# Seven-product FFN: gate sums, a weight sum and a cast listed sooner, other PSUM banks for group 0's down product, last rows of h split by token halves

## Chip, cores and metric

The kernel runs on one core of a Trainium2 chip. Its time is the device time of one execution in microseconds (us); three timed runs of the kernel before are at hand, and one execution under the profiler.

## The reference

One decoder layer on 512 tokens of width 1024, in float32: an FFN, a token-mixing part, a second FFN, a gated embedding (PLE) and a norm.

```python
def rmsnorm(x, g):
    xf = x.astype(jnp.float32)
    y = xf * lax.rsqrt(jnp.mean(xf * xf, axis=-1, keepdims=True) + EPS)
    return (y * g.astype(jnp.float32)).astype(x.dtype)

def swiglu(x, w_gate, w_up, w_down):
    return (jax.nn.silu(x @ w_gate) * (x @ w_up)) @ w_down
...
        h = h + 0.5 * swiglu(rmsnorm(h, ffn1_norm[i]), ffn1_w_gate[i], ffn1_w_up[i], ffn1_w_down[i])
        n = rmsnorm(h, mix_norm[i])
        proj = n @ w_in[i]
...
        h = h + jnp.concatenate([ya, yb], axis=-1) @ w_out[i]
        h = h + 0.5 * swiglu(rmsnorm(h, ffn2_norm[i]), ffn2_w_gate[i], ffn2_w_up[i], ffn2_w_down[i])
        gate = jax.nn.sigmoid(rmsnorm(h, ple_norm[i]) @ ple_w_gate[i] + ple_b_gate[i])
        h = h + gate * (p[i] @ ple_w_proj[i])
    return rmsnorm(h, final_norm)
```

The hidden width of each FFN, D_FF, is 2816, or 11 groups of 256.

## The kernel before

**Float32 by parts.** Each operand of a product is split into a rounded part (hi) and a remainder (lo). A weight tile that a DMA has brought in (raw, rawb or s) is cast to `whi` on ScalarE (ACT, line 515) and `wlo = raw - whi` is made on VectorE (DVE, line 519); TensorE (PE) then adds three products, whi with x's hi, whi with x's lo, wlo with x's hi.

**The FFN's groups.** Group 0 is computed plainly (`plain_steps`). Groups 1 to 10 compute gate and up halves of two token halves with seven block products instead of eight (`Group.steps`), one step each, 24 matmuls of 128x256 (line 731), in the order 1, 7, 6, 4, 5, 2, 3 (group 1 of the first FFN is "turned": 1, 7, 2, 6, 4, 5, 3). Three PSUM accumulators belong to a group: x (steps 1, 2), q (steps 7, 4), both from the three "mm" banks, and a (steps 6, 5, 3), of which there are two, used by alternate groups. Step 1 ends with a copy of x into a, the seed (line 853); p7 and u2 are kept copies (lines 857, 861). The weights of step 6 are w11 plus a sum s1, those of step 3 that plus w12. These sums are made in place on DVE (line 741: `add(w11.raw, self.s1)`, `add(w11.raw, w12.raw)`); s1 itself and step 7's weights are made by accumulating DMAs on GpSimd's (POOL's) queue (lines 749 and 746).

**The gate.** `gate_sum(0)` (line 874, G<-mm,u) needs q after step 4 and u2; `gate_sum(1)` (line 874, G<-a,p) needs a after step 5 and p7. Step 3 adds into the same a bank, so PE's step 3 waits for `gate_sum(1)`. `gate(half)` scales (line 879, DVE) and applies Silu (line 881, ACT); `times_r` (line 885), and `finish` (line 890, at even groups of the second half also line 894) follow.

**Order.** PE, ACT, DVE and SyncE execute what the program lists, in that order. `run` walks through the steps and lists, around a step's product, the cast of the step two ahead, what follows the products before it (`after`), the wlo of later steps (`split`), weight sums (`sums`) and the tasks attached by `also` (`post`). The first FFN's first steps are listed by hand, in the string `ENTRY` (product11 is step 3 of the turned group; after9 belongs to its step 4, and so on).

**Down products.** Group 0's part of the down product takes four steps of two products each (`down`, matmuls at line 231, sums into h at line 930): steps 0 and 2 write two small-pool banks "sm", steps 1 and 3 two "mm" banks. The first block of the rest of the down product (`blocks_down`, 35 steps, line 1096), also on seven products, writes sm. It forms its own operands from G on ACT and DVE (line 1023).

**The rows of h.** At the end of each FFN, h is finished row block by row block. Each of the eight is scaled by the next norm and split (`scaled_split`: ACT line 199, DVE line 200), squared (line 273, ACT) and summed (line 274, GpSimd or DVE) for the norm. Blocks 4 to 7 are done one by one while step 3 of `blocks_down` runs; blocks 0 to 3 follow after its last product (`upper_done`), all 512 tokens at a time. Only the second token half of blocks 0 to 3 is changed by that last product (`add_to(0, k, 1, "a", ...)`); the first half is final at the first step of it (`add_to(0, 1, 0, "x", ...)`).

```python
        def upper_done():
            for k in range(2):
                add_to(0, k, 1, "a", ALU.add)
                yield
            yield from parts_of_h(range(NP))
```

What follows the second FFN is the PLE gate: products with x (line 231), a sum over the squares (line 284), the norm's scale (lines 240 to 308), and its spread over partitions (line 321).

## Time and profile before

| | |
|---|---|
| timed runs | 1071.28, 1065.8, 1065.92 us; median 1065.92 |
| profiled execution | 1069.35 us; span of its profile 1067.6 us |
| granted TensorE clock, mean | 0.991 |
| DVE idle for ACT's whi, line 519 of raw tiles | 64.9 us |
| ACT idle ahead of the Silu, line 881 | 134.9 us |

A row of a timeline has the start from the span's begin, the length in us, the engine, line and operation, what it writes and reads, and in brackets the engine's idle time ahead of it with what ended that. A row of the waits has who waited for whom, us in total, how often, and the longest. A row of windows has the stretch, its length, the busy time of PE, PE's weight loads, DVE, ACT and POOL with the counts of instructions, then the granted clock, the DMA engines' busy share and GB/s. A row of DMA issues ends with the KB of each and the median us from issue to landing.

### The profile page before, as it was taken

The page shows a single profiled execution, that of the slowest core. Times are in us where ns is not written, and L with a number is a line of the kernel's source. Part 1 is how long each engine was busy: PE and PEld are TensorE (multiplying, and loading weights), DVE is VectorE, ACT ScalarE, POOL GpSimd, SP SyncE. Part 2 cuts the span into 40 slices and gives each one's busy share as a digit, 9 for nine tenths or more (in the row PEclk, how much of TensorE's full clock was granted, in tenths as well). Part 3 has the DMA queues.
Part 4 walks back from the last instruction along what each step waited for, and adds up shares of the span by engine and source line. Part 5 has one row for each costly group of instructions (what it writes and reads, how often), then busy time and mean ns, then how long its engine had stood idle before and what let it go on. Part 6 is the DMA issues. An engine that isn't in the chain of part 4 may idle for free. (4 is left out here: it accounts for less than half of the span.)

```text
span 1067.6 us, 18352 instructions
## 1 busy us (share of the span) xinstructions
PE 1027.9 (96%) x7472; PEld 958.0 (90%) x7472; DVE 848.2 (79%) x1104; ACT 574.2 (54%) x764; POOL 151.9 (14%) x145
## 2 busy tenths in 40 slices
PE   9989999999999999999999999999999999999996
PEld 7889999998999899888888888889999998999886
DVE  7968778778898787776998757677778778998866
ACT  7644544545666465575754434454444446576654
POOL 0101001000320300134333000000010000330311
PEclk9989999999999999999999999999999999999988
DMA  9957667626992143444532325755676543995312
GB/s 339 314 138 212 183 159 204 177 64 240 226 233 63 58 126 90 155 144 133 148 110 72 107 86 185 173 144 163 185 192 178 167 130 144 263 211 152 131 47 80
DMA packets 51765, 168.90 MB, mean 158 GB/s; under 512 B 5856, under 2 KB 6368, under 8 KB 51680
## 3 DMA queue, kind: packets, MB, share of 16 engines
q1 hardware_dynamic: 38864, 123.61, 34.2%
q0 software_dynamic: 11520, 41.95, 20.6%
q10 hardware_dynamic: 1296, 2.16, 0.6%
q8 instruction: 58, 0.95, 0.4%
q14 instruction: 27, 0.22, 0.1%
HBM read 163.44 MB, written 4.26 MB: 157 GB/s over the span
## 5 line engine op out<-in xcount | busy, mean ns | idle before, releaser
L519 DVE TENSOR_TENSOR wlo<-raw,whi 128x1024 fp32r<-128x1024 f32 (+3 forms) x166 | 201.1, 1212 | 65.1 <-ACT whi L515 64.9
L515 ACT CAST whi<-raw 128x1024 fp32r<-128x1024 f32 (+3 forms) x166 | 166.8, 1011 | 127.1 <-PE a L217 24.0
L731 PE MATMUL mm<-xfb,whi 128*128 128x256 f32 x960 | 163.9, 275 | 0.0
L731 PEld LDWEIGHTS mm<-xfb,whi 128*128 128x128 f32 x960 | 145.8, 192 | 0.0
L731 PE MATMUL mm<-xfb,wlo 128*128 128x256 f32 x480 | 132.1, 275 | 0.0
L519 DVE TENSOR_TENSOR wlo<-rawb,whi 128x1024 fp32r<-128x1024 f32 x76 | 92.9, 1222 | 49.2 <-ACT whi L515 49.1
L731 PE MATMUL a<-xfb,whi 128*128 128x256 f32 x640 | 115.7, 284 | 14.5 <-ACT G L881 10.7
L731 PEld LDWEIGHTS a<-xfb,whi 128*128 128x128 f32 x640 | 98.8, 195 | 21.0 <-ACT G L881 13.7
L515 ACT CAST whi<-rawb 128x1024 fp32r<-128x1024 f32 x76 | 79.4, 1047 | 55.4 <-DVE rawb L741 31.7
L881 ACT ACTIVATE G<-G 128x512 f32<-128x512 f32 x40 | 25.2, 630 | 134.9 <-DVE G L879 134.9
L731 PE MATMUL a<-xfb,wlo 128*128 128x256 f32 x320 | 90.9, 284 | 5.4 <-DVE wlo L519 5.4
L731 PEld LDWEIGHTS mm<-xfb,wlo 128*128 128x128 f32 x480 | 92.2, 192 | 0.1
L1096 PE MATMUL a<-xfb,whi 128*128 128x256 f32 x480 | 80.7, 275 | 0.0
L746 POOL DMA_DIRECT2D raw<-in_ffn_gu x20 | 17.2, 861 | 430.0 <-DMA raw<-in_ffn_gu 254.4
L1096 PEld LDWEIGHTS a<-xfb,whi 128*128 128x128 f32 x480 | 72.8, 192 | 0.0
L731 PEld LDWEIGHTS a<-xfb,wlo 128*128 128x128 f32 x320 | 62.3, 195 | 8.9 <-DVE wlo L519 8.9
L217 PE MATMUL sm<-x,whi 128*128 128x512 f32 x224 | 68.4, 387 | 0.0
L1096 PE MATMUL a<-xfb,wlo 128*128 128x256 f32 x240 | 66.0, 275 | 0.0
L1096 PE MATMUL sm<-xfb,whi 128*128 128x256 f32 x320 | 54.3, 276 | 2.4 <-DVE h L930 2.4
L274 POOL TENSOR_TENSOR ssum<-ssum,tmp 128x512 f32<-128x512 f32 x26 | 38.6, 1484 | 117.6 <-ACT tmp L273 116.9
L731 PE MATMUL a<-xfa,whi 128*128 128x256 f32 x320 | 54.7, 275 | 0.1
L731 PE MATMUL mm<-xfa,whi 128*128 128x256 f32 x320 | 54.7, 275 | 0.0
(411 smaller groups left out, 2642.8 us busy)
## 6 DMA issues: line engine op xcount, KB each, us to landing
raw<-in_ffn_gu SPq DMA_DIRECT2D x56, 512.0 KB, 4.7
rawb<-in_ffn_gu SPq DMA_DIRECT2D x32, 512.0 KB, 7.6
raw<-in_w_in SPq DMA_DIRECT2D x28, 512.0 KB, 3.6
s<-in_ffn_gu SPq DMA_DIRECT2D x20, 512.0 KB, 5.9
raw<-in_ffn_gu POOLq DMA_DIRECT2D x20, 512.0 KB, 7.8
s<-in_ffn_gu POOLq DMA_DIRECT2D x20, 512.0 KB, 9.6
rawb<-in_ffn_dw POOLq DMA_DIRECT2D x18, 512.0 KB, 9.5
raw<-in_w_out SPq DMA_DIRECT2D x16, 512.0 KB, 3.3
```

Source lines behind the costliest of these rows:

```text
L217: nc.tensor.matmul(ps, w, turned(x), start=first and n == 0, stop=last and n == 2, skip_group_check=True)
L274: self.engines[i].tensor_tensor(self.totals[i], self.totals[i], sq, ALU.add)
L515: nc.scalar.copy(self.hi[:, c], self.raw[:, c])
L519: nc.vector.tensor_tensor(self.lo[:, c], self.raw[:, c], self.hi[:, c].bitcast(F32), ALU.subtract)
L731: nc.tensor.matmul(o, wt[:, c], turned(xt), start=fresh and p == m == n == 0, stop=last and n == 2, skip_group_check=True,)
L746: nc.gpsimd.dma_start(w21.raw, self.src[0], accum_op=ALU.add)
L881: nc.scalar.activation(t, t, AF.Silu)
L1096: nc.tensor.matmul(o, wt[:, c], xt, start=i in (1, 7) and t == jj == n == d % 2 == 0, stop=t == nt - 1 and jj == 1 and d % 2 == 1 and n == ...
```

## The change

The change edits the listing at six places. No product is added or taken away, and PE's order stays the same but for the names of banks.

1. The two gate sums of a group stand together, and the scaling and Silu of half 0 behind them.
2. The weight sum for step 3 is listed after step 6's product (ahead of step 2's wlo) instead of among the `sums` two steps later.
3. Step 6's cast becomes a task of its own (`cast`), which `run` lists ahead of what follows step 3 of the group before (its Silu of half 1).
4. Group 0's down product uses mm and a for step 0, sm for step 1, mm for steps 2 and 3.
5. Blocks 0 to 3 of h are split, squared and summed by token halves: half 0 in `post` tasks of the last steps of `blocks_down`, half 1 where all was before. ACT has 16 rows more in the program, DVE 8, GpSimd 8.
6. In `ENTRY`, the weight sum of step 3 of the turned group comes right behind after9, and its cast and wlo (split12) ahead of product11.

The core of the diff:

```diff
-split10 split10.1 load13 product9 split11 load14 product10 after9 after10
-after10.1:1 product11 after11
+split10 split10.1 load13 product9 split11 load14 product10 after9 after9.1 after10
+after10.1:1 split12 product11 after11
...
-    def scaled_split(h, name, k):
-
-        hi = sb("x", dt=F32R)
-        lo = sb("x", dt=F32R)
-        nc.scalar.activation(hi, h[k], AF.Copy, scale=col(name, k))
+    def scaled_split(h, name, k, tok=slice(0, T), to=None):
+
+        hi, lo = to or (sb("x", dt=F32R), sb("x", dt=F32R))
+        nc.scalar.activation(hi[:, tok], h[k][:, tok], AF.Copy, scale=col(name, k))
         nc.vector.scalar_tensor_tensor(
-            lo, h[k], col(name, k), hi.bitcast(F32), ALU.mult, ALU.subtract
+            lo[:, tok], h[k][:, tok], col(name, k), hi[:, tok].bitcast(F32), ALU.mult, ALU.subtract
         )
...
-                gates[0] = gates[0][0],
-                gates[1] = gates[1][0][:1],
+                gates[0] = [lambda: self.gate_sum(0)],
+                gates[1] = [lambda: self.gate_sum(1), lambda: self.gate(0)],
...
-                    (6, w11, None, "a", False, (), lambda: add(w11.raw, self.s1), (self.keep_u2,)),
+                    (6, w11, None, "a", False, (), lambda: add(w11.raw, self.s1), ([self.keep_u2, lambda: add(w11.raw, w12.raw)],)),
...
-                    (3, w11, None, "a", False, (), lambda: add(w11.raw, w12.raw), (lambda: self.finish(1),) if self.turned else ([up, lambda: self.gate(1)],)),
+                    (3, w11, None, "a", False, (), None, (lambda: self.finish(1),) if self.turned else ([up, lambda: self.gate(1)],)),
...
+            alone = i == 6 and not self.turned
+
             def split():
-                yield from w.split_by_engine(self.s1 if raw else None, kept=parts)
+                if alone:
+                    w.low()
+                    parts[0] = w.hi, w.lo
+                else:
+                    yield from w.split_by_engine(self.s1 if raw else None, kept=parts)
...
+            if alone:
+                s.cast = w.cast
...
-                    ps[d] = bank("mm", 3) if i % 2 else sm_ps()
+                    ps[d] = sm_ps() if i == 1 else acc_ps() if d == D_ORDER[1] else bank("mm", 3)
...
-            yield from parts_of_h(range(NP))
+            yield from parts_of_h(range(NP), halves[1])
...
+        for t, ds in ((1, (0,)), (2, (1,)), (3, (2, 3))):
+            also(made[3][t], "post", lambda ds=ds: parts_of_h(ds, halves[0]))
```

How this moves instructions is shown at three places. Rows give the line (in the changed kernel a line in this part of the code is up to 10 lower down or one higher up), the operation, what it writes and reads, and the tile's size.

DVE in group 8 of the first FFN, from step 2's wlo and the weight sum for step 3 to the scaling of half 1. mm_2104 is q, a_269 the group's a bank, rawb_2038 is w12, raw_249 is w11. Before:

```order
L519 TENSOR_TENSOR wlo_2201<-rawb_2038,whi_2200 128x1024
L741 TENSOR_TENSOR raw_249_1873<-raw_249_1873,rawb_2038 128x1024
L519 TENSOR_TENSOR wlo_2230<-raw_249_1873,whi_2229 128x1024
L874 TENSOR_TENSOR G_628<-mm_2104,u_283_2198 128x2x256
L879 SCALAR_TENSOR_TENSOR G_628<-G_628,rall_488 128x2x256
L874 TENSOR_TENSOR G_628<-a_269_2069,p_280_2167 128x2x256
L519 TENSOR_TENSOR wlo_2262<-rawb_2102,whi_2261 128x1024
L885 SCALAR_TENSOR_TENSOR G_628<-G_628,rall_488 128x2x256
L519 TENSOR_TENSOR wlo_2293<-raw_2135,whi_2292 128x1024
L741 TENSOR_TENSOR rawb_2102<-rawb_2102,s_278_2138 128x1024
L890 TENSOR_TENSOR G_628<-G_628,mm_2070 128x2x256
L879 SCALAR_TENSOR_TENSOR G_628<-G_628,rall_488 128x2x256
```

and in the changed kernel:

```order
L740 TENSOR_TENSOR raw_249_1873<-raw_249_1873,rawb_2038 128x1024
L518 TENSOR_TENSOR wlo_2202<-rawb_2038,whi_2201 128x1024
L518 TENSOR_TENSOR wlo_2230<-raw_249_1873,whi_2229 128x1024
L881 TENSOR_TENSOR G_629<-mm_2104,u_283_2198 128x2x256
L881 TENSOR_TENSOR G_629<-a_269_2069,p_280_2167 128x2x256
L886 SCALAR_TENSOR_TENSOR G_629<-G_629,rall_488 128x2x256
L518 TENSOR_TENSOR wlo_2262<-rawb_2102,whi_2261 128x1024
L892 SCALAR_TENSOR_TENSOR G_629<-G_629,rall_488 128x2x256
L518 TENSOR_TENSOR wlo_2293<-raw_2135,whi_2292 128x1024
L740 TENSOR_TENSOR rawb_2102<-rawb_2102,s_278_2138 128x1024
L897 TENSOR_TENSOR G_629<-G_629,mm_2070 128x2x256
L886 SCALAR_TENSOR_TENSOR G_629<-G_629,rall_488 128x2x256
```

The weight sum (raw_249 with rawb_2038) went ahead of step 2's wlo, and the sum that reads a_269 ahead of the scaling of half 0. ACT, in the same group and the next step 6 (raw_249 here is w11 with s1 added, its cast whi_2098 or whi_2095; the Silus are G). Before:

```order
L881 ACTIVATE G_628<-G_628 128x2x256
L515 CAST whi_2033<-raw_249_1873 128x1024
L515 CAST whi_2064<-raw_1906 128x1024
L881 ACTIVATE G_628<-G_628 128x2x256
L515 CAST whi_2098<-raw_249_1873 128x1024
L853 COPY a_269_2069<-mm_2070 128x512
```

and in the changed kernel:

```order
L888 ACTIVATE G_629<-G_629 128x2x256
L514 CAST whi_2033<-raw_249_1873 128x1024
L514 CAST whi_2064<-raw_1906 128x1024
L514 CAST whi_2095<-raw_249_1873 128x1024
L888 ACTIVATE G_629<-G_629 128x2x256
L860 COPY a_269_2069<-mm_2070 128x512
```

The cast of step 6's weights changed places with the Silu of half 1, and both stand ahead of the seed copy a_269. DVE at the entry, in group 1 of the first FFN, where rawb_171 is w11, mm_502 is q and a_98 the a bank. Before:

```order
L519 TENSOR_TENSOR wlo_587<-s_57_216,whi_586 128x1024
L874 TENSOR_TENSOR G_628<-mm_502,u_116_622 128x2x256
L879 SCALAR_TENSOR_TENSOR G_628<-G_628,rall_488 128x2x256
L874 TENSOR_TENSOR G_628<-a_98_458,p_107_553 128x2x256
L741 TENSOR_TENSOR rawb_171<-rawb_171,rawb_282 128x1024
L519 TENSOR_TENSOR wlo_658<-rawb_171,whi_657 128x1024
L519 TENSOR_TENSOR wlo_662<-raw_110_560,whi_661 128x1024
```

and in the changed kernel:

```order
L518 TENSOR_TENSOR wlo_587<-s_57_216,whi_586 128x1024
L740 TENSOR_TENSOR rawb_171<-rawb_171,rawb_282 128x1024
L881 TENSOR_TENSOR G_629<-mm_502,u_116_622 128x2x256
L886 SCALAR_TENSOR_TENSOR G_629<-G_629,rall_488 128x2x256
L518 TENSOR_TENSOR wlo_633<-rawb_171,whi_632 128x1024
L881 TENSOR_TENSOR G_629<-a_98_458,p_107_553 128x2x256
L518 TENSOR_TENSOR wlo_662<-raw_110_560,whi_661 128x1024
```

The weight sum moved from behind the second gate sum to ahead of the first, and its wlo to ahead of the second. Last, DVE in group 0's down product of the first FFN; h_94 to h_97 are parts of h, to which each of the four steps adds its two products, and sm, mm and a are the banks that are read. Before:

```order
L519 TENSOR_TENSOR wlo_2780<-raw_2625,whi_2779 128x512
L930 TENSOR_TENSOR h_94<-sm_2762,h_94 128x512
L930 TENSOR_TENSOR h_96<-sm_2769,h_96 128x512
L519 TENSOR_TENSOR wlo_2800<-raw_2658,whi_2799 128x512
L885 SCALAR_TENSOR_TENSOR G_628<-G_628,rall_488 128x2x256
L1023 TENSOR_TENSOR xfb_2804<-G_628,xfb_2804 128x1024
L930 TENSOR_TENSOR h_94<-mm_2783,h_94 128x512
L930 TENSOR_TENSOR h_96<-mm_2790,h_96 128x512
L519 TENSOR_TENSOR wlo_2822<-rawb_2660,whi_2821 128x1024
L890 TENSOR_TENSOR G_628<-G_628,a_317_2526 128x2x256
L894 TENSOR_TENSOR G_628<-G_628 128x512
L930 TENSOR_TENSOR h_95<-sm_2807,h_95 128x512
```

and in the changed kernel:

```order
L518 TENSOR_TENSOR wlo_2780<-raw_2625,whi_2779 128x512
L937 TENSOR_TENSOR h_94<-mm_2762,h_94 128x512
L937 TENSOR_TENSOR h_96<-a_347_2769,h_96 128x512
L518 TENSOR_TENSOR wlo_2800<-raw_2658,whi_2799 128x512
L892 SCALAR_TENSOR_TENSOR G_629<-G_629,rall_488 128x2x256
L1030 TENSOR_TENSOR xfb_2804<-G_629,xfb_2804 128x1024
L937 TENSOR_TENSOR h_94<-sm_2783,h_94 128x512
L937 TENSOR_TENSOR h_96<-sm_2790,h_96 128x512
L518 TENSOR_TENSOR wlo_2822<-rawb_2660,whi_2821 128x1024
L897 TENSOR_TENSOR G_629<-G_629,a_317_2526 128x2x256
L901 TENSOR_TENSOR G_629<-G_629 128x512
L937 TENSOR_TENSOR h_95<-mm_2807,h_95 128x512
```

No row moved here; only the banks changed. The fourth step's second product is mm_2838, and it lies in the bank of mm_2807 (three mm banks in turn: 2807, 2814, 2831), so its first matmul waits for the row h_95<-mm_2807.

More of the change, by code (lines that the diff above doesn't have):

```diff
@@ L263, in __init__, with add @@
             self.n = 0
-        def add(self, src):
+        def add(self, src, tok=slice(0, T)):
             i = self.n % len(self.engines)
@@ L271, in add @@
             else:
-                sq = tmp()
-                nc.scalar.activation(sq, src, AF.Square)
-                self.engines[i].tensor_tensor(self.totals[i], self.totals[i], sq, ALU.add)
+                sq, t = tmp()[:, tok], self.totals[i][:, tok]
+                nc.scalar.activation(sq, src[:, tok], AF.Square)
+                self.engines[i].tensor_tensor(t, t, sq, ALU.add)
         def sums(self, more=None):
@@ L696, in splitter, with done @@
         x += [None] * ND
-        def done(d):
-            x[d] = scaled_split(h, name, d)
+        def done(d, tok=slice(0, T)):
+            x[d] = scaled_split(h, name, d, tok, x[d])
         return done
@@ L1057, in seeds, with parts_of_h @@
                 yield
-        def parts_of_h(ds, then=None):
+        def parts_of_h(ds, tok=slice(0, T)):
             for d in ds:
-                after(d)
+                after(d, tok)
                 yield
-                out_norm.add(h[d])
+                out_norm.add(h[d], tok)
                 yield
```

## The prediction

> **What bounds the kernel now.** I read the page's busy shares first, then PE's waits, then two windows that hold the product groups (groups 2 to 10 of the first FFN, 1 to 10 of the second), and at last one group on the timeline.
>
> ```profile
> PE 1027.9 (96%) x7472; PEld 958.0 (90%) x7472; DVE 848.2 (79%) x1104; ACT 574.2 (54%) x764; POOL 151.9 (14%) x145
> PE a L731 <- ACT G L881: 10.7, 19, 2.2
> PE a L731 <- DVE wlo L519: 5.4, 18, 0.5
> ...
> 64.56:246.69 182.13, 175.21 (x1514) 170.70 (x1513) 139.46 (x154) 86.50 (x109) 12.65 (x15) 1.00 0.58 157
> 691.50:895.97 204.47, 195.00 (x1681) 189.75 (x1680) 159.98 (x182) 97.33 (x124) 13.77 (x16) 1.00 0.56 154
> ```
>
> TensorE (PE) is busy 96% of the span, so only its waiting can be won. The two wait rows have the count of the groups: 19 times "ACT G L881", 18 times wlo. Their idle (10.7 + 5.4) understates the loss, since ends of pipelined matmuls are modelled; starts are not. So I measure by starts. On PE, the first matmuls of steps 6 (191.26), 5, 2 and 3 of one group of the first FFN and of step 6 of the next (211.59):
>
> ```profile
> 191.26 0.38 PE L731 MATMUL a<-xfb,whi 128*128 128x256 f32 x1
> 197.28 0.39 PE L731 MATMUL a<-xfa,whi 128*128 128x256 f32 x2
> 199.96 0.39 PE L731 MATMUL mm<-xfb,whi 128*128 128x256 f32 x2
> 203.27 0.46 PE L731 MATMUL a<-xfb,whi 128*128 128x256 f32 x2 [0.47 <-ACT G L881]
> 211.59 0.49 PE L731 MATMUL a<-xfb,whi 128*128 128x256 f32 x2
> 212.37 0.38 PE L731 MATMUL a<-xfb,wlo 128*128 128x256 f32 x1 [0.29 <-DVE wlo L519]
> ```
>
> A step that waits for nothing takes 199.96 - 197.28 = 2.68 us; seven take 18.76, and the group takes 20.33. So 1.57 us per group are lost: step 3 starts at 203.27 instead of 202.64 (0.63), and the rest, 0.94, lies at step 6 (its bank's seed copy, then its wlo). Over the windows: 182.13 - 9 x 18.76 = 13.3 us, and 204.47 - 10 x 18.76 = 16.9 us.
>
> Who is late? VectorE (DVE) and ScalarE (ACT) in the same group:
>
> ```profile
> 197.56 1.22 DVE L741 TENSOR_TENSOR raw<-raw,rawb 128x1024 f32<-128x1024 f32 x1
> 199.97 1.23 DVE L519 TENSOR_TENSOR wlo<-raw,whi 128x1024 fp32r<-128x1024 f32 x1 [1.19 <-ACT whi L515]
> 201.11 0.68 DVE L874 TENSOR_TENSOR G<-mm,u 128x512 f32<-128x512 f32 x1
> 202.44 0.69 DVE L874 TENSOR_TENSOR G<-a,p 128x512 f32<-128x512 f32 x1
> ...
> 202.56 0.63 ACT L881 ACTIVATE G<-G 128x512 f32<-128x512 f32 x1 [2.62 <-DVE G L879]
> 209.49 0.63 ACT L881 ACTIVATE G<-G 128x512 f32<-128x512 f32 x1 [4.42 <-DVE G L879]
> 210.02 1.03 ACT L515 CAST whi<-rawb 128x1024 fp32r<-128x1024 f32 x1
> 210.96 0.58 ACT L853 COPY a<-mm 128x512 f32<-128x512 f32 x1
> ```
>
> Step 3 writes the a bank that G<-a,p reads. That sum ends at 203.13, and PE moves; the Silu that PE's row names ends near it but holds no bank. DVE reached the sum late, because it idled 1.19 us for the cast behind the weight sum (L741) and then did G<-mm,u and its scaling first. At step 6 ACT stands idle 4.42 us before a Silu; only behind it come the cast of step 6's weights and the seed copy (to 211.54; PE starts at 211.59).
>
> **The groups (edits 1 to 3).** No work is added there; each edit lists something sooner that is ready. Take step 6's start as zero and a step each 2.68 us: steps 6, 4, 5 and 2 end at 2.68, 5.36, 8.04 and 10.72, where step 3 starts. The weight sum goes ahead of step 2's wlo, and so the cast behind it runs under that wlo and the 1.19 us go. G<-mm,u runs 7.7 to 8.4 and G<-a,p 8.4 to 9.1, which is 1.6 ahead of step 3. The scaling and the Silu end at 9.7 and 10.3, then the cast of the next step 1 at 11.2 and its wlo at 12.4 (wanted at 13.6 by that step's third matmul: slack 1.1). Step 6's cast runs 15.3 to 16.3 in ACT's old idle, the Silu ends at 17.1, the seed copy at 17.6 (wanted at 18.76), the wlo at 17.7 (wanted at 19.0). What is late next is the wlo of step 1, and it is in time. DVE's load allows it: 139.46 / 9 = 15.5 us a group of 18.76. I take the whole loss, **-13.3 and -16.9**; the bounds are none left and 0.5 us a group left (19 x 0.5 = 9.5).
>
> **The entry (edit 6).** DVE and PE about step 3 of the first FFN's group 1, and two windows:
>
> ```profile
> 52.97 0.69 DVE L874 TENSOR_TENSOR G<-mm,u 128x512 f32<-128x512 f32 x1 [1.70 <-issue]
> 58.60 0.79 PE L731 MATMUL a<-xfb,whi 128*128 128x256 f32 x2 [3.05 <-ACT whi L515]
> 59.86 0.58 PE L731 MATMUL a<-xfb,wlo 128*128 128x256 f32 x1 [0.47 <-DVE wlo L519]
> 64.56 0.39 PE L731 MATMUL mm<-xfa,whi 128*128 128x256 f32 x2
> ...
> 54.15:57.56 3.41, 1.41 (x13) 1.22 (x11) 2.06 (x3) 0.05 (x1) 0.00 (x0) 1.00 0.00 0
> 57.56:64.39 6.83, 5.32 (x23) 5.03 (x24) 5.81 (x7) 3.40 (x4) 0.84 (x1) 0.50 0.74 250
> ```
>
> The weight sum moves into the 1.70 us of DVE idle ahead of 52.97, its cast to about 52.5, its wlo ahead of G<-a,p, which then ends at about 56.3 and releases step 3's bank: PE starts at 56.35. Step 3 also took 64.56 - 58.60 = 5.96 us at a granted clock of 0.50. With under 1 us of idle I expect the full clock and an end at 56.35 + 2.68 = 59.03: **-5.5**. If the clock falls anyhow, -2.7.
>
> **Group 0's down product (edit 4).** DVE keeps its order; the banks change. DVE, PE's wait and the whole stage in the first FFN:
>
> ```profile
> 250.70 0.69 DVE L519 TENSOR_TENSOR wlo<-raw,whi 128x512 fp32r<-128x512 f32 x1 [1.21 <-ACT whi L515]
> 258.83 1.28 DVE L930 TENSOR_TENSOR h<-sm,h 128x512 f32<-128x512 f32 x2
> 259.57 0.49 PE L1096 MATMUL sm<-xfb,whi 128*128 128x256 f32 x2 [1.21 <-DVE h L930]
> 246.69:273.39 26.70, 24.77 (x171) 22.54 (x169) 25.46 (x30) 15.27 (x14) 5.11 (x6) 1.00 0.95 305
> ```
>
> Before, the third pair of sums into h (258.83) held the sm bank of the first block: 1.21 us of idle. Those banks are now free early, but the fourth step's second product takes the mm bank of the third step's first product, and that bank's sum is the first of the same third pair. DVE works without a gap from 250.70 to there, so the sum ends about 12.4 us after the stage's start (12.7 before, less some 0.3, as the gate's work ahead comes sooner). PE, which does the four steps in 10.4, wants the bank at 3.5/4 of that, 9.06: **a new idle of 3.4**. It replaces the 1.21 and, as DVE gets ahead meanwhile, the later waits for wlo (1.5); the stage grows by 3.4 - 1.2 - 1.5 or so, **+0.5 each, +1.0** in all (bounds -2.9 each, the stage's whole loss, and +1.5).
>
> The clock comes on top. An idle of 2.16 us did not halve it, the 3.05 did, and so did the two waits for x near the end:
>
> ```profile
> 710.24 0.46 PE L731 MATMUL a<-xfb,whi 128*128 128x256 f32 x2 [2.16 <-ACT G L881]
> 706.10:709.51 3.41, 1.98 (x18) 1.78 (x16) 2.54 (x4) 0.80 (x1) 0.00 (x0) 1.00 0.74 202
> 1009.88:1013.30 3.42, 1.90 (x10) 1.30 (x9) 2.50 (x2) 0.35 (x1) 1.87 (x2) 1.00 0.93 324
> 1013.30:1020.12 6.82, 6.82 (x20) 5.64 (x20) 4.47 (x16) 0.70 (x1) 0.00 (x0) 0.50 0.21 79
> ```
>
> The half clock began at 57.56 and 1013.30, 955.74 apart, which is 280 times 3.413; so I cut the idle stretches on that grid. Cells with 1.41 and 1.90 us of PE work were followed by the half clock, one with 1.98 was not. An idle of 3.4 leaves at most 1.71 in one of the cells that it touches, wherever it falls: both stages should halve. The price of one, at the entry: 5.96 - 2.68 - 0.47 = 2.8 us. **+5.6.**
>
> The Trainium skill, TensorE: Matmul & The Clock Gate, Part 1, has the half rate come after at least one idle window of about 3.4 us on a free-running grid. If that means a window without work, no idle here fills one and the sum has no +5.6. The trace speaks against this reading: 1.41 us of work stood in the cell before 57.56.
>
> **The rows of h by halves (edit 5).** At the second FFN's end (one wait row for two stalls, then PE), and at the first's:
>
> ```profile
> PE mm L231 <- DVE x L200: 1.5, 2, 0.8
> 1014.23 0.77 PE L231 MATMUL a<-x,whi 128*128 128x512 f32 x1
> 1019.49 0.63 PE L231 MATMUL mm<-x,whi 128*128 128x512 f32 x1
> 363.73 0.48 PE L217 MATMUL sm<-x,wlo 128*128 128x512 f32 x1 [1.08 <-DVE wlo L519]
> ```
>
> Half of four rows' splits goes under the last products, so x is there in time and the 1.5 go. Twelve matmuls took 1019.49 - 1014.23 = 5.26 us at clock 0.50 instead of 2.59; with the stalls gone that 2.7 goes too. The added half instructions on ACT stand ahead of the next weights' casts and give some 0.7 back: **-3.5** (bounds -1.5 and -5). At the first FFN's end the 1.08 and what the modelled ends hide: **-1.6** (0 to -1.9). The output projection's first a bank turns out the other of two, with a later reader: +0.2.
>
> **Sum**, against the profiled execution of 1069.35 us: -5.5 - 13.3 - 16.9 + 1.0 - 1.6 - 3.5 + 0.2 = -39.6, so 1029.7, and with the clock's +5.6 **1035.3**. The median of the runs, 1065.92, is 3.4 lower, about the price of one halving. I don't subtract it, since the old halvings are taken out already.
>
> **Rivals.** (a) The idle is there but the clock holds in one stage or in both (a phase of the grid, or the 3.4 is 2.5): 1032.5 or 1029.7; against it the 1.90 row. This is where the skill's rule, read as above, would end. (b) The groups keep about 0.5 us each, since the wlo of step 1 now stands behind two sums, a scaling and a Silu with 1.1 of slack: 1035.3 + 9.5 = 1044.8. For it, DVE's 15.5 of 18.76; against it, that DVE's waits in the group are all for ACT. (c) The new bank wait stays short, as PE's third step or the casts pace it: no halving, and -1.2 instead of +0.5 in each stage: 1029.7 - 3.4 = 1026.3. (d) The listing isn't what holds the groups, but the pace of the weight transfers: 1035.3 + 13.3 + 16.9 = 1065.5. Against it, the DMA share of 0.58. (e) Slower: step 6's cast now stands on ACT ahead of the Silu and the seed copy. It needs the sum with s, which needs the accumulating transfer of s (POOL's queue, issued once the sum before has read s):
>
> ```profile
> 207.03 1.22 DVE L741 TENSOR_TENSOR rawb<-rawb,s 128x1024 f32<-128x1024 f32 x1
> 208.42 0.86 POOL L749 DMA_DIRECT2D s<-in_ffn_gu  x1 [0.85 <-DVE rawb L741]
> s<-in_ffn_gu POOLq DMA_DIRECT2D x20, 512.0 KB, 9.6
> ```
>
> Now the next sum comes 20.33 after 207.03, 18.9 after the issue; with shorter groups 17.4. A landing beyond that, and past the seed's slack of 1.2, delays Silu, seed and PE together: with 9.6 it is far off; from 18.6 on it decides, and at 20.6 it costs 19 x 2.0 = 38 us: 1073.
>
> **Chances.** Forecast 0.42, (a) 0.22, (b) 0.18, (c) 0.12, (d) 0.03, (e) 0.03. The range, 1023 to 1046, holds the forecast, (a), (b) and (c), with the bounds of the ends. About 0.5% (5.3 us) is what a measurement of this kernel can tell from no change: faster by more than that 0.94, within it 0.03 (d), slower 0.03 (e).
>
> **What would show it.** Right: groups 18.8 apart, no PE wait on G or wlo in bank a; under 1 us of idle near 56 and clock 1.00 there; in each down product one PE wait of about 3.4 us on a sum into h, and a half clock behind it; no wait for x near the end. Wrong: a period over 19.2 (b), or near 20.3 (d); no down wait (c); ACT idle for a transfer ahead of step 6's cast (e).

## The result, and the profile after

The changed kernel takes 1037.54 us (median of 4 runs, 1036.18 to 1038.16) against 1066.74 before: a ratio of 0.9716 (95% interval 0.9686 to 0.9746). The forecast was 1035.3, range 1023 to 1046. Its profiled execution took 1037.41 us. The page of the changed kernel: TensorE's 96% are now 98%.

```profile
span 1035.7 us, 18386 instructions
PE 1012.8 (98%) x7472; PEld 952.4 (92%) x7472; DVE 847.8 (82%) x1112; ACT 580.2 (56%) x780; POOL 154.7 (15%) x153
PEclk9999999998999999999999999999999999999999
```

PE's waits in the changed kernel (who waited for whom, us in total, times, longest). The two rows of the groups, 19 and 18 waits before, are gone but for one wait, that of the turned group in the entry (the last row here); two new rows head the list:

```profile
PE mm L230 <- DVE h L937: 6.7, 2, 3.4
PE mm L230 <- DVE wlo L518: 2.2, 1, 2.2
...
PE a L730 <- DVE G L881: 0.9, 1, 0.9
```

Windows of the changed kernel, cut at the same places of the program as in the prediction (length, busy PE, weight loads, DVE, ACT, POOL, granted clock, DMA share, GB/s): groups 2 to 10 of the first FFN, its down stage and its end, then the second FFN's groups, its down stage and its end.

```profile
58.68:227.52 168.84, 168.84 (x1515) 168.84 (x1513) 140.61 (x156) 88.54 (x109) 12.81 (x15) 1.00 0.63 171
227.52:257.70 30.18, 26.81 (x170) 24.79 (x169) 25.91 (x30) 15.19 (x14) 5.12 (x6) 0.89 0.98 296
338.10:350.41 12.31, 11.64 (x50) 8.60 (x49) 10.95 (x13) 5.11 (x11) 5.13 (x7) 1.00 0.32 95
676.22:864.57 188.35, 188.22 (x1682) 187.82 (x1680) 159.02 (x182) 99.29 (x124) 13.81 (x16) 1.00 0.61 167
864.57:893.58 29.01, 25.70 (x171) 23.68 (x169) 25.90 (x30) 15.42 (x14) 5.22 (x6) 0.94 0.97 300
973.98:988.48 14.50, 12.01 (x60) 9.81 (x58) 12.51 (x26) 6.40 (x12) 5.00 (x6) 1.00 0.67 227
```

168.84 us is 9 x 18.76 to the last digit: none of these nine groups waits at all. The down stages grew from 26.70 and 26.59 to 30.18 and 29.01, at clocks of 0.89 and 0.94. By stage, from the starts of PE's steps in the two profiles (us):

| stage | before | after | difference | forecast |
|---|---|---|---|---|
| up to group 2 (entry) | 64.56 | 58.68 | -5.88 | -5.5 |
| groups 2 to 10, first FFN | 182.13 | 168.84 | -13.29 | -13.3 |
| its down stage | 26.70 | 30.18 | +3.48 | +0.5 + 2.8 |
| its end | 12.20 | 12.31 | +0.11 | -1.6 |
| mixing part | 325.51 | 325.81 | +0.30 | +0.2 |
| groups, second FFN | 204.47 | 188.35 | -16.12 | -16.9 |
| its down stage | 26.59 | 29.01 | +2.42 | +0.5 + 2.8 |
| its end, to the norm's spread | 16.95 | 14.50 | -2.45 | -3.5 with the rest |
| rest | 47.69 | 47.22 | -0.47 | |

The rest of each down product, between the down stage and the end, took 80.40 us in both kernels and both FFNs. The sum is -31.9, where the forecast had -34.0. Four single places of the changed kernel answer to the rows of before. First, one group on DVE and ACT: the second gate sum ends at 223.12, which is 9.0 us after step 6's start at 214.12 (9.1 was worked out), and step 3 starts at 224.84 without a wait.

```profile
214.12 0.39 PE L730 MATMUL a<-xfb,whi 128*128 128x256 f32 x2
224.84 0.39 PE L730 MATMUL a<-xfb,whi 128*128 128x256 f32 x2
...
222.44 0.68 DVE L881 TENSOR_TENSOR G<-a,p 128x512 f32<-128x512 f32 x1
223.75 0.63 ACT L888 ACTIVATE G<-G 128x512 f32<-128x512 f32 x1 [3.09 <-DVE G L886]
```

Second, the new wait in the down product, with its releaser on DVE:

```profile
240.12 1.22 PE L230 MATMUL mm<-xfa,whi 128*128 128x512 f32 x2 [3.37 <-DVE h L937]
239.38 1.28 DVE L937 TENSOR_TENSOR h<-mm,h 128x512 f32<-128x512 f32 x2
```

And windows of the cells around the two halvings; a cell is one stretch of 3.41 us of the grid on which the prediction cut the idle. 1.10 and 0.24 us of PE work stood in the cells ahead of them. In the first FFN the halved cell itself had only 2.35 us of work and a second halved cell followed (239.06 to 245.88); in the second FFN it was full, and the clock came back after one.

```profile
235.65:239.06 3.41, 1.10 (x6) 0.62 (x4) 3.38 (x6) 2.47 (x2) 0.62 (x1) 1.00 1.03 412
239.06:242.47 3.41, 2.35 (x6) 1.90 (x7) 3.41 (x5) 0.00 (x0) 0.60 (x2) 0.50 1.03 407
873.94:877.35 3.41, 0.24 (x1) 0.24 (x2) 3.38 (x6) 1.18 (x2) 0.88 (x1) 1.00 1.02 412
877.35:880.76 3.41, 3.41 (x12) 2.87 (x12) 3.41 (x4) 1.31 (x2) 0.88 (x1) 0.50 1.05 369
```

Third, the second FFN's end. The waits for x are gone, and a longer one for the next weights' wlo has come. DVE reached that wlo late, since six splits of x ahead of it (two whole rows, four halves) took 6.94 us, while GpSimd summed squares beside them:

```profile
968.62 6.94 DVE L199 SCALAR_TENSOR_TENSOR x<-h,vec,x 128x512 fp32r<-128x512 f32 x6
975.48 1.21 DVE L518 TENSOR_TENSOR wlo<-raw,whi 128x1024 fp32r<-128x1024 f32 x1
968.36 6.92 POOL L273 TENSOR_TENSOR ssum<-ssum,tmp 128x512 f32<-128x512 f32 x6 [1.35 <-ACT tmp L272]
976.75 0.48 PE L230 MATMUL mm<-x,wlo 128*128 128x512 f32 x1 [2.17 <-DVE wlo L518]
```

The clock stayed full behind this wait (1.00 in the stage's window), though the cell in which it lies had only 1.66 us of PE work:

```profile
972.92:976.33 3.41, 1.66 (x13) 1.25 (x12) 3.41 (x5) 2.78 (x3) 2.20 (x3) 1.00 0.00 0
```

Fourth, the entry: step 3 of the turned group starts at 55.93, where 56.35 was worked out and 58.60 stood before.

```profile
55.93 0.46 PE L730 MATMUL a<-xfb,whi 128*128 128x256 f32 x2 [0.88 <-DVE G L881]
```

### The profile page after: what moved, and what is told of

It reads as the page before. It is cut to its first block, busy times and chain, and to the rows that moved or that the text cites. A ratio compares the mean times of both kernels' runs of the same rounds, so it can differ in the third digit from the quotient of the medians.

```text
span 1035.7 us, 18386 instructions
## 1 busy us (share of the span) xinstructions
PE 1012.8 (98%) x7472; PEld 952.4 (92%) x7472; DVE 847.8 (82%) x1112; ACT 580.2 (56%) x780; POOL 154.7 (15%) x153
## 3 DMA queue, kind: packets, MB, share of 16 engines
q10 hardware_dynamic: 1296, 2.16, 0.6%
## 4 chain that ended last, share of the span: by engine, by line
PE 82%; DVE 11%; ACT 2%; issue 2%; DMA 1%; SPq 0%; POOL 0%; DVEq 0%; ACTq 0%; POOLq 0%
PE mm L730 20%; PE a L730 15%; PE a L1103 7%; PE sm L1103 5%; PE sm L216 5%; PE mm L1103 5%; PE mm L230 5%; PE mm L216 5%; PE a L216 4%; DVE wlo L518 3%; PE a L230 2%; PE sm L230 2%; PE sm L824 1%; PE a L824 1%; PE mm L824 1%
## 5 line engine op out<-in xcount | busy, mean ns | idle before, releaser
L730 PE MATMUL a<-xfb,whi 128*128 128x256 f32 x640 | 109.4, 275 | 0.9 <-DVE G L881 0.9
L730 PE MATMUL a<-xfb,wlo 128*128 128x256 f32 x320 | 88.0, 275 | 0.0
L1103 PE MATMUL a<-xfb,whi 128*128 128x256 f32 x480 | 80.7, 275 | 0.0
L1103 PE MATMUL a<-xfb,wlo 128*128 128x256 f32 x240 | 66.0, 275 | 0.0
L273 POOL TENSOR_TENSOR ssum<-ssum,tmp 128x512 f32<-128x512 f32 (+1 forms) x34 | 40.9, 1202 | 114.8 <-ACT tmp L272 113.3
```

The source lines that it names most:

```text
L273: self.engines[i].tensor_tensor(t, t, sq, ALU.add)
L730: nc.tensor.matmul(o, wt[:, c], turned(xt), start=fresh and p == m == n == 0, stop=last and n == 2, skip_group_check=True,)
L1103: nc.tensor.matmul(o, wt[:, c], xt, start=i in (1, 7) and t == jj == n == d % 2 == 0, stop=t == nt - 1 and jj == 1 and d % 2 == 1 and n == ...
```

## The experiments

Each is the changed kernel with one thing altered. Their medians come from several chips; the kernel before, run beside them, had medians from 1066.1 to 1070.3. So between kernels that ran on different chips a difference under some 4 us says nothing, and lengths of stages in the profiles are used there.

A halved cell can also come and go without an edit at its place. Nine profiles, the changed kernel's among them, have the same wait of 2.2 us for wlo at the second FFN's end (2.17 to 2.20). In four of them (the changed kernel, e4, e7, e8) the clock stays full and the stage takes 14.5 us; in five (e1, e2, e3, e5, e6) one cell is halved and it takes 16.0 to 16.1. The cell ahead of the halving in e1:

```profile
967.15:970.56 3.41, 1.23 (x8) 0.82 (x8) 3.41 (x5) 2.09 (x3) 1.59 (x2) 1.00 0.00 0
```

**The down product: banks, DVE or clock?** Three kernels. The first (e1) undoes edit 4:

```diff
-                    ps[d] = sm_ps() if i == 1 else acc_ps() if d == D_ORDER[1] else bank("mm", 3)
+                    ps[d] = bank("mm", 3) if i % 2 else sm_ps()
```

> The changed kernel with edit 4 undone (group 0's down product writes sm, mm, sm, mm as before). Theory A, that the wait of 3.4 us for a sum into h and the half clock behind it come from the new banks: the waits of 3.4 go, an idle of about 1.2 us on the first block comes back, the clock stays full, and the stage takes 26.7 us (before) instead of 30.2 and 29.0 in the two FFNs, so the time is 3.5 + 2.4 less than the changed kernel's 1037.5: 1031.6 (1030 to 1033). Theory B, that the stage is limited by DVE and the place of the wait doesn't matter: a wait of about the same length moves to the blocks, the clock drops there too, and the time stays at 1037.

It took 1032.71 us, 4.8 less than the changed kernel. Its two down stages:

```profile
227.74:254.20 26.46, 24.52 (x171) 22.61 (x169) 25.22 (x30) 15.33 (x14) 5.11 (x6) 1.00 0.95 307
860.75:887.14 26.39, 24.43 (x171) 22.70 (x169) 24.91 (x30) 15.37 (x14) 5.21 (x6) 1.00 0.96 310
```

They are about as long as before the change (26.70 and 26.59), at full clock, with the wait of 1.2 us on the first block back. They are 3.7 and 2.6 us shorter than in the changed kernel, where theory A has 3.5 and 2.4; the whole time gains less, since this profile has the halved cell at the second FFN's end. So edit 4 costs what theory A says, and the rest of the change doesn't need it.

The second (e2) gives the waiting product another bank:

```diff
+                    if d == D_ORDER[7]:
+                        ps[d] = kept_acc[0]
+                        accumulate(ps[d], (w.hi, w.lo), 2 * k, groups[0].out)
+                        continue
                     ps[d] = sm_ps() if i == 1 else acc_ps() if d == D_ORDER[1] else bank("mm", 3)
+                    if d == D_ORDER[1]:
+                        kept_acc.append(ps[d])
```

> The changed kernel, but the down product's fourth step writes its second product into the bank of step 0's second product (the a bank, whose sum into h is the second of all) instead of the mm bank of the third step. Theory A: that bank is free 5.7 us after the stage's start and wanted at 9.1, so the wait goes, no block waits for sm either, only about 1 us remains for wlo that DVE still makes late; the stage takes 24.5 to 25.5 us instead of 30.2 and 29.0, the time is 1028 to 1030. Theory B, the stage is limited by DVE: the stage stays at 26.7 or above, 1032 or more.

It took 1032.01 us. No product waits for a bank any more, and yet the stages take 26.39 and 26.29 us, nothing less than with the old banks: four waits for wlo have come in the place of the bank waits.

```profile
PE sm L1111 <- DVE wlo L518: 3.8, 4, 1.2
```

The 24.5 to 25.5 of theory A was wrong; theory B, with 26.7 or above, was nearer. That DVE's own work (25 us of these 26.4) sets the stage's length is argued from the waits, which moved and did not shrink; no run took work off DVE here. The 1032 agrees with theory B only with the halved cell at the second FFN's end, which this profile has too.

The third (e3) keeps edit 4 and fills its wait with matmuls whose results nobody uses:

```diff
+                    if d == D_ORDER[7]:
+                        spare = sm_ps(), sm_ps()
+                        for s in (0, 0, 1):
+                            accumulate(spare[s], (w.hi, w.lo), 0, groups[0].out)
```

> The changed kernel with 18 matmuls of 128x512 added in each down product, ahead of the waiting product, into the sm banks that the first block overwrites; their results are used by nothing. They keep TensorE busy for about 3.3 of the 3.4 us of the wait (and at most 0.9 us of them lies past it). If the half clock comes from the idle stretch alone, the granted clock stays 1.00 in both stages and the stage takes 27 to 28 us instead of 30.2 and 29.0: the time is 1033 to 1035. If the clock's fall has another cause (the load of transfers in that stage), it stays at 0.5 there and the time is 1037 to 1039.

It took 1035.38 us, 2.2 less than the changed kernel, with 18 matmuls more in each FFN and with the halved cell at the second FFN's end. The stages:

```profile
228.09:255.74 27.65, 27.65 (x189) 25.88 (x188) 26.00 (x30) 15.76 (x14) 5.11 (x6) 1.00 0.96 304
862.59:890.24 27.65, 27.65 (x189) 25.88 (x188) 25.96 (x30) 15.66 (x14) 5.21 (x6) 1.00 0.97 305
```

Full clock in both, at the same load of transfers (0.96 against 0.98): it was the idle stretch that halved the clock. The clock's price is thus 30.18 - 27.65 = 2.5 us in the first FFN, with two halved cells, and 1.4 in the second, with one (a little more, since the filling itself ends late). The wait alone makes the stage at most 27.65; 27.2 was forecast. A profile below (e10) has the wait at full clock without any filling: 27.43.

**The groups: which edit does it?** Four kernels. The first (e4) undoes edits 1 and 2 (the latter in all groups that aren't turned) and keeps the cast:

```diff
-                gates[0] = [lambda: self.gate_sum(0)],
-                gates[1] = [lambda: self.gate_sum(1), lambda: self.gate(0)],
+                gates[0] = gates[0][0],
+                gates[1] = gates[1][0][:1],
...
-                    (6, w11, None, "a", False, (), lambda: add(w11.raw, self.s1), ([self.keep_u2, lambda: add(w11.raw, w12.raw)],)),
+                    (6, w11, None, "a", False, (), lambda: add(w11.raw, self.s1), ([self.keep_u2, lambda: add(w11.raw, w12.raw)],) if self.turned else (self.keep_u2,)),
...
-                    (3, w11, None, "a", False, (), None, (lambda: self.finish(1),) if self.turned else ([up, lambda: self.gate(1)],)),
+                    (3, w11, None, "a", False, (), None if self.turned else lambda: add(w11.raw, w12.raw), (lambda: self.finish(1),) if self.turned else ([up, lambda: self.gate(1)],)),
```

> The changed kernel with edits 1 and 2 undone in all groups that aren't turned; edit 3, the cast of step 6 by itself, stays. Theory A, one chain from the end of step 6 over the copy u, the cast and wlo of step 2, the weight sum, the cast and wlo of step 3, the two gate sums: it takes 8.3 us from the start of the copy u as in the kernel before, and ends 0.5 us after step 3 could start; loss of 0.5 us in each of 19 groups, 1047. Theory B, each edit saves the idle that stood at its own place, so step 3's loss of 0.63 comes back whole and nothing of step 6's: 19 x 0.63 = 12, 1049.5. Theory C, step 3 was late only since step 6 was: no loss, 1037.5.

It took 1053.81 us. Step 3 waits in each group as before the change, step 6 no longer, and the period of the groups is 211.86 - 192.39 = 19.47:

```profile
192.39 0.46 PE L730 MATMUL a<-xfb,whi 128*128 128x256 f32 x2 [0.47 <-ACT G L888]
211.86 0.46 PE L730 MATMUL a<-xfb,whi 128*128 128x256 f32 x2 [0.47 <-ACT G L888]
```

The chain of theory A has its 8.28 us here too (copy u at 203.44, end of G<-a,p at 211.72), but 0.2 was missing in it: the 0.14 us from the sum's end to PE's start and a slower start of the step, which make 0.71 per group where 0.5 was expected. Some 4 us more lie in group 1 of the second FFN, whose step 3 starts 2.3 late and runs in part at the half clock. So theory B's 0.63 was nearer than A's 0.5, for steady groups; theory C falls.

Then each edit alone was undone. Edit 1 (e5, the first hunk above alone):

> The changed kernel with edit 1 alone undone (the scaling of half 0 again between the two gate sums; edits 2 and 3 stay). Theory A, one chain with slack: in the changed kernel the second gate sum ends 9.0 us after step 6's start and step 3 wants it at 10.7; 0.6 later is still in time, so groups stay at 18.76 and the time at 1037.5. Theory B, each edit saves the idle at its own place: 0.6 per group come back, 19 x 0.6 = 11, 1049.

1038.31 us, and the groups stay at 18.76 (168.85 us for groups 2 to 10; 188.50 for those of the second FFN, against 188.35): theory A. Edit 2 (e6, the other two hunks alone):

> The changed kernel with edit 2 alone undone in the groups that aren't turned (the weight sum of step 3 again behind step 2's wlo; edits 1 and 3 stay). Theory A: with the scaling behind both sums the chain that took 8.28 us from the copy u takes 7.7, so the second gate sum ends 10.6 us after step 6's start, just at the 10.7 that step 3 wants; loss of 0 to 0.1 per group, 1037.5 to 1039.5. Theory B: its idle of 1.19 us on DVE comes back as 0.6 per group or more: 1049.

1056.01 us. Theory A falls. The 1.19 us of theory B stand on DVE again, but the groups lose more than its 0.6 each: 6.8 us in the first FFN and 8.7 in the second, 0.8 per group. That is nearly as much as with edits 1 and 2 both undone (groups 2 to 10 of the first FFN take 175.67 us here, 9 x 19.47 = 175.2 there). The period is 19.8 and 19.3 in turn. PE's waits, and DVE, ACT and PE in one group:

```profile
PE a L730 <- DVE G L881: 4.6, 10, 1.4
PE mm L730 <- DVE wlo L518: 3.7, 17, 0.2
```

```profile
211.95 0.68 DVE L881 TENSOR_TENSOR G<-a,p 128x512 f32<-128x512 f32 x1
214.86 1.23 DVE L518 TENSOR_TENSOR wlo<-raw,whi 128x1024 fp32r<-128x1024 f32 x1 [1.63 <-ACT whi L514]
213.26 0.64 ACT L888 ACTIVATE G<-G 128x512 f32<-128x512 f32 x1 [3.09 <-DVE G L886]
216.14 0.38 PE L730 MATMUL mm<-xfa,wlo 128*128 128x256 f32 x1 [0.23 <-DVE wlo L518]
```

With the weight sum late the two gate sums are late together: the second ends at 212.63, 11.1 us after step 6's start at 201.52, against 9.0 in the changed kernel. Behind them come the scaling, the Silu, the next step 1's cast and its wlo, and PE now waits there too, at 216.14: 17 times in the kernel, beside ten waits for a gate sum at step 3 (one of them the entry's). This is the mechanism of rival (b), which the changed kernel escapes by the time that edit 2 wins. So edit 1 without edit 2 moves much of the wait into the next group, and with edit 2 it is hardly needed.

Edit 3 (e7):

```diff
-            alone = i == 6 and not self.turned
+            alone = False
```

> The changed kernel with edit 3 alone undone (step 6's cast again behind the Silu of half 1; edits 1 and 2 stay). Theory A: the scaling of half 1 now ends 2.2 us ahead of step 6's start, since the groups' other work comes sooner; the Silu, the cast and the seed copy end at step 6's start, the wlo 0.4 to 0.5 us late: 19 x 0.45 = 8.6, 1046. Theory B: step 6 loses the whole 0.94 of the kernel before: 19 x 0.94 = 18, 1055.

1050.19 us, 12.7 more: between the theories. The groups of both FFNs take 13.3 us more. Groups 2 to 10 of the first FFN take 174.73 us, a loss of 0.65 per group on the average, at step 6's start (the seed copy, in every second group) and above all at its third matmul, which waits for wlo:

```profile
220.46 0.38 PE L730 MATMUL a<-xfb,wlo 128*128 128x256 f32 x1 [0.28 <-DVE wlo L518]
```

**The entry.** Edit 6 undone (e8: the old two lines of the order, and the turned group's weight sum among its `sums`):

```diff
-split10 split10.1 load13 product9 split11 load14 product10 after9 after9.1 after10
-after10.1:1 split12 product11 after11
+split10 split10.1 load13 product9 split11 load14 product10 after9 after10
+after10.1:1 product11 after11
```

> The changed kernel with edit 6 undone (the turned group's weight sum behind both gate sums, its cast and wlo behind that). If the edit took away 3 us of idle and the half clock behind it: 5.9 us more, 1043.4, with the clock at 0.5 after the idle. If the clock's fall there depends on the grid's phase and doesn't come: 3.1 more, 1040.6.

1043.91 us. The idle of 3 us is back and the half clock with it, this time for one cell:

```profile
58.30 0.49 PE L730 MATMUL a<-xfb,whi 128*128 128x256 f32 x2 [3.04 <-ACT whi L514]
59.56 0.38 PE L730 MATMUL a<-xfb,wlo 128*128 128x256 f32 x1 [0.77 <-DVE wlo L518]
```

The window of that cell:

```profile
60.06:63.47 3.41, 3.41 (x18) 3.41 (x18) 3.41 (x5) 0.60 (x1) 0.83 (x1) 0.50 0.77 298
```

**The rows of h.** Edit 5 undone (e9):

```diff
-            yield from parts_of_h(range(NP), halves[1])
+            yield from parts_of_h(range(NP))
...
-        for t, ds in ((1, (0,)), (2, (1,)), (3, (2, 3))):
-            also(made[3][t], "post", lambda ds=ds: parts_of_h(ds, halves[0]))
```

> The changed kernel with edit 5 undone (blocks 0 to 3 of h split, squared and summed whole, after the last product). By the stages of the two profiles: the first FFN's end gives 0.1 us back, the second's loses 2.5 to 2.9, a part of it a half clock that depends on the grid: 1037.5 + 2.6 = 1040 (1037 to 1041). If the halves' new wait of 2.2 us for wlo costs as much as the two waits for x that they took away, the time stays at 1037.5.

1037.7 us: nothing lost. The first FFN's end takes 12.19 us (12.31 with the edit). The second FFN's end has its two waits for x again, as before the change, and is still 0.3 us shorter than the changed kernel's 14.50:

```profile
972.89:987.09 14.20, 12.36 (x60) 9.74 (x58) 12.21 (x23) 6.63 (x10) 6.22 (x4) 1.00 0.77 259
978.41:981.82 3.41, 2.44 (x10) 1.24 (x8) 3.41 (x3) 0.16 (x1) 3.20 (x3) 1.00 0.96 299
```

The second of the waits on PE:

```profile
982.37 0.48 PE L230 MATMUL mm<-x,whi 128*128 128x512 f32 x1 [0.76 <-DVE x L199]
```

Before the change the two waits fell so that one cell had 1.90 us of work, and the clock halved; here the cell on the first of them has 2.44, and it holds. What this stage gained from before to after (16.95 to 14.50) is the missing halving. Edit 5 does not keep it away: with the edit, five of the nine profiles named above have a halved cell there. This profile also has one in its last part, at 1019.38, which the changed kernel's has not (the rest takes 47.98 us against 47.22), and one fewer in the first down stage (29.05 against 30.18); so the stages, and not the whole times, show what the edit costs: 0.3 us at the second FFN's end and 0.1 at the first's.

Why do the halves not gain? Two kernels move GpSimd's sums. First (e10), squares and sums of the first halves are made later:

```diff
-                out_norm.add(h[d], tok)
-                yield
+                if tok != halves[0]:
+                    out_norm.add(h[d])
+                    yield
```

> The changed kernel, but the first token halves of blocks 0 to 3 are only split early; their squares and sums are made with the second half's, as whole rows after the last product. GpSimd then has 4 sums fewer (of 256 columns) beside the early splits. Theory A, GpSimd's sums stretch the DVE instructions that run beside them (six splits took 6.9 us in the second FFN's end where 2 x 0.73 + 4 x 0.40 = 3.1 would do): the six splits take 5 us or less, the wlo comes in time or under 1 us late instead of 2.2, and the time falls by 1.5 to 2: 1035.8. Theory B, the wlo is late since its cast stands behind the halves on ACT: the splits stay near 6.9 us or the wait stays at 2.2 less the 1.6 that ACT is freed of, and the time falls by under 1.

1039.09 us, no gain. The wlo is in time now, but the four half splits behind the last product stand beside GpSimd's four whole sums and take 1.4 us each, and PE waits three times for x (1.2 us) and once for h (0.5; stage 14.73):

```profile
966.61 4.25 DVE L199 SCALAR_TENSOR_TENSOR x<-h,vec,x 128x512 fp32r<-128x512 f32 x4
976.18 5.73 DVE L199 SCALAR_TENSOR_TENSOR x<-h,vec,x 128x256 fp32r<-128x256 f32 x4
```

Theory A had the early part nearly right (4.25 + 0.47 + 0.47 = 5.2 us for the six) and its time wrong: the stretch moved with the sums. This profile shows one thing more, in the second FFN's down stage. PE waits 3.40 us there for the same sum into h, the two cells on which the wait falls have 1.74 and 1.68 us of PE work, and the clock stays full:

```profile
864.14:891.57 27.43, 24.03 (x170) 22.39 (x169) 25.95 (x30) 15.51 (x14) 5.22 (x6) 1.00 0.97 306
871.63:875.04 3.41, 1.74 (x9) 1.18 (x7) 3.41 (x5) 2.94 (x2) 0.00 (x0) 1.00 1.03 420
875.04:878.45 3.41, 1.68 (x9) 1.52 (x10) 3.38 (x6) 0.29 (x1) 0.88 (x1) 1.00 1.03 407
```

Second (e11), the halves' sums are made on DVE itself:

```diff
-                self.engines[i].tensor_tensor(t, t, sq, ALU.add)
+                (nc.vector if tok != slice(0, T) else self.engines[i]).tensor_tensor(t, t, sq, ALU.add)
```

> The changed kernel, but the sums of token halves (16 of 256 columns) are made on DVE instead of GpSimd; ACT's work is as before, DVE has 0.4 us more for each, 6.4 in all, 3.2 in each FFN's end. Theory A (GpSimd's sums stretch DVE's instructions): the early splits and their sums together take no longer than the six splits alone did, 5 us or less, and the wait of 2.2 us for wlo falls under 1: the time falls by 1 to 2 in spite of the added DVE work, 1036. Theory B (ACT's order): DVE's added work comes on top, and the time rises by 1 to 3: 1039.

1034.45 us, 3.1 less, with 16 instructions more on DVE. Its half splits take 0.47 us each, its sums 0.41, and the second FFN's end 13.45 us:

```profile
966.70 2.16 DVE L199 SCALAR_TENSOR_TENSOR x<-h,vec,x 128x512 fp32r<-128x512 f32 x2
976.47 0.47 DVE L199 SCALAR_TENSOR_TENSOR x<-h,vec,x 128x256 fp32r<-128x256 f32 x1
976.86 0.41 DVE L273 TENSOR_TENSOR ssum<-ssum,tmp 128x256 f32<-128x256 f32 x1
```

The window of that end:

```profile
972.45:985.90 13.45, 12.00 (x58) 9.99 (x58) 10.95 (x30) 6.53 (x12) 0.00 (x0) 1.00 0.71 233
```

By the stages, the ends give 1.3 us (the first, 11.01) and 1.05, and the blocks ahead of the second take 0.4 more (80.79 against 80.40): 2.0 of the 3.1 in all. Another 1.1 is one halved cell fewer in the first down stage (29.05), which the edit does not touch. So theory A holds for the mechanism, with a gain at its upper bound. The six splits with their four sums took 6.4 us (966.70 to 973.08) and not under 5; four of the six, the two whole ones and a half one behind each, still took 2.16 per pair, beside two whole sums on GpSimd. The wait for wlo fell from 2.2 to 1.1.

**Both together** (e12): e2's bank and e11's sums.

> The changed kernel with the edits of e2_reuse_bank and e11_sums_on_dve together: the down product's fourth step reuses the a bank of its first, and the sums of token halves are made on DVE. They act in stages that are apart, so if each works as its own run shows, the gains add: e2 was 5.5 below the changed kernel, e11 3.1; 1037.5 - 5.5 - 3.1 = 1028.9 (1028 to 1030). If the two runs gained by the same thing (the clock's phase), the sum is less: 1032.

1029.74 us (1029.34 to 1030.24), a ratio of 0.9633 to the kernel before (0.9620 to 0.9647), 7.8 us under the changed kernel. The clock stays full up to 1022.8 us of 1028.3. The two gains add to 8.6, so 0.8 of it is missing; the entry in this profile, which no edit here touches, is 1.0 longer than the changed kernel's (59.68 against 58.68).

## Why the prediction was right or wrong

**Right: the groups.** The forecast was to win all of 30.2 us there; it was 29.4, and groups 2 to 10 of the first FFN have no wait left. The missing 0.8 lies in groups 1 and 2 of the second FFN (19.09 and 19.18 us). In group 1 DVE also forms operands between the weights' steps (684.49 to 687.50); that this is the cause is argued and not tested. The second gate sum held to 0.1 us of the time worked out by hand (9.0 against 9.1). What the prediction did not say, and e5 to e7 show, is how the gain divides: by the lengths of the groups, undoing edit 2 costs 15.5, edit 3 13.3 and edit 1 0.2, 29.0 together, so edits 2 and 3 make nearly all of the 29.4.

**Right, in part by luck: the new bank wait.** 3.37 and 3.31 us where 3.4 was worked out, and the half clock behind both. The stage without the clock took 27.43 in e10, against 27.2. One term of its sum was misread: the 1.5 us of waits for wlo are the total of two FFNs, 0.7 in each, so the sum gives +1.5 per stage and not +0.5; in the second FFN e10 shows +0.84 (27.43 against 26.59). The clock's price of 2.8 was about right for two halved cells (2.5) and double the real one for a single cell (1.4). The step "both stages should halve", wherever the idle falls, does not hold: in e10 the same idle left 1.74 and 1.68 us in its cells and the clock stayed full. Of the 18 such stages in nine profiles 17 were halved, so the forecast was the likely case and rival (a) a possible one. The reading of the Trainium skill (TensorE: Matmul & The Clock Gate, Part 1: half rate after at least one idle window) by which only a window without work counts is out: 1.10 us of work in the cell ahead of 239.06 did not save the clock.

**Right: the entry.** -5.88 against -5.5, and with edit 6 undone 4.9 of it come back (from step 5's start to group 2: 52.41 to 63.74, against 52.21 to 58.68), by the idle and one halved cell.

**Wrong: the rows of h.** The step that failed reads: "Half of four rows' splits goes under the last products, so x is there in time and the 1.5 go ... with the stalls gone that 2.7 goes too." The 1.5 did go, but 2.2 came for wlo; and the 2.7 went without the edit (e9), by where the waits fell on the clock's grid. That it is gone in the changed kernel is luck: five kernels with the edit have a halved cell there, at 1.6 us. The -3.5 and -1.6 of this part were in truth +0.3 and +0.1 for the edit, and -2.7 for the clock. The term that failed is what the early half splits cost on DVE ahead of the next wlo: the prediction put it at nothing and counted only 0.7 for ACT. They stretch beside GpSimd's sums: at the changed kernel's second FFN's end seven half splits beside a sum take 0.94 to 0.95 us each, and the eighth, with no sum beside it (983.24), 0.47. In e11, with the sums of the halves off GpSimd, the wait for wlo is 1.1; those 1.1 stay with the splits and the sums in DVE's own queue. The kernel before had shown the stretch at its own end, where four whole splits took 1.7 us each beside GpSimd's sums:

```profile
1005.57 6.81 DVE L200 SCALAR_TENSOR_TENSOR x<-h,vec,x 128x512 fp32r<-128x512 f32 x4
1005.38 6.45 POOL L274 TENSOR_TENSOR ssum<-ssum,tmp 128x512 f32<-128x512 f32 x4 [4.88 <-ACT tmp L273]
```

Its shortest whole split took 0.73. The Trainium skill, SBUF — State Buffer, "SBUF: two separate sides", has the two engines share a port pair that one of them locks for a whole instruction, if the DVE instruction has two SBUF inputs and GpSimd's reads SBUF; the run with the sums on DVE agrees (the median of all 24 splits is 0.95 us in the changed kernel, 0.48 there). Which instruction waited for which was not measured.

The forecast came within 2.2 us because the errors partly cancel, and because no cell was halved at the second FFN's end. The errors: 1.7 and 0.6 too much gain at the ends and 0.8 in the groups, against 0.9 too much loss in the second down stage and 0.4 too little gain at the entry.

## What to carry to other kernels

Work out a chain in microseconds against the time at which its end is wanted; an edit that shortens it is worth something only up to there, so the second edit on a chain that already ends in time wins next to nothing. Where a halved clock can come and go, compare stages and not whole times. When banks are moved, write down for each bank the instruction that frees it and where that stands in the queue of its engine, before counting the wait that goes. Cost an instruction by a row in which the same neighbours run; a step that is split into halves can meet them twice.

## What the runs showed of the hardware

The clock's halving goes by how the idle lies on a grid of 3.41 us, and not by its length alone. The same wait of 2.2 us (2.17 to 2.20) at the second FFN's end was followed by the half clock in five profiles and not in four; an idle of 3.40 us left the clock full in e10, and two waits of 0.76 us within 1.7 us of each other halved it in the kernel before and left it full in e9.

By PE's work as the profile counts it, cells with 0.24, 0.99, 1.10, 1.23 and 1.41 us were followed by the half clock; cells with 1.50 (e8, from 978.25), 1.66 (the changed kernel, from 972.92), 1.68 and 1.74 (e10), 1.98 (before) and 2.44 (e9) were not. But 1.90 in the kernel before (from 1009.88) was followed by it, and so were cells behind the second FFN with up to 2.35, such as 2.34 in e9 (from 1015.97). These two hold matmuls with results of 128x1 (lines 284 and 1964); whether their work is counted too high, or PE's work isn't what decides, isn't shown.

A halved cell that was itself full of work was followed by full clock in e8 and in the second FFN of the changed kernel; one with 2.35 us of work by a second halved cell. In the kernel before, 1013.30 to 1020.12 was full by the profile and halved for two cells: that isn't explained.

A split of a 128x512 row on DVE took 0.73 us at the shortest and 1.7 beside GpSimd's sums; a half of it took 0.47 with the sums on DVE (e11) and 1.4 beside GpSimd's whole sums (e10).
